# A planned two-layer encoder on one Trainium2 core: a later early group, its forms in the order of their use, a ScalarE copy and longer rests

## The chip, the cores and the metric

The kernel runs on one core of a Trainium2 chip. Its time is the device time of one execution in microseconds (us), and the figure to compare is the median of several runs. TensorE (PE) multiplies; VectorE (DVE), ScalarE (ACT) and GpSimd (POOL) do the rest; transfers are issued from the queue of SyncE (SP) and from that of POOL. The engines run asynchronously, each through its own queue in order, and wait for one another by semaphores.

## The reference

Two layers of a hybrid encoder for 256 tokens of width 2048. The part that matters here:

```python
h = rms_norm(x, norm_g)
u = h @ w_in                       # 4 branches' q, k, v, gates, an indexer, 4 x 2048 gate columns
y_a = sparse_index_attention(...)  # the indexer picks 64 keys a query
y_b = retention(...)
y_c = head_rms_norm(hgrn2(f, heads(c_i), heads(c_q)), hgrn_g)
y_m = memory_attention(...)
for n, (y, z) in enumerate(((y_a, a_z), (y_b, b_z), (y_c, c_z), (y_m, m_z))):
    branch = y.reshape(B, S, W).astype(dt) * jax.nn.silu(z)
    merged = merged + jax.nn.sigmoid(gate_all[:, :, n]) * (branch @ w_branch[n])
return x + merged @ w_out
```

All of it is float32, and weights dominate: each layer reads its own input projection (2048 x 15944), its branch projections and its output projection.

## The kernel before

**Arithmetic.** A float32 product is made of three passes in a reduced format: each operand is cut into a high part, which ScalarE rounds, and a low part, which VectorE subtracts, and TensorE adds high x high, high x low and low x high. Activations are the stationary operand, in 128 x 128 pieces; weights stream. The normalised input stands transposed in four blocks of four pieces, `x00`..`x03` in layer 0 and `x10`..`x13` in layer 1, each with an `h` and an `l` tile.

**Weights.** A slab is 512 rows x 512 columns (some 256 or 328 columns wide), loaded as `raw` by SP into one of four buffers. It is cut in two halves into `whi` and `wlo`, of which there are four each. `gemm_plan` fixes the order of all slabs in advance. `advance` follows each half that TensorE has been given: it pumps the stream and then cuts the half that comes four later. So the cast of that later half waits, on ScalarE's queue, for TensorE to have finished the half just issued.

**Tasks.** Everything beside the plain matmuls is a generator in `Stream.tasks`. `pump` counts a tick per half (half a tick for half a product, which is given twelve matmuls in two halves), sends up to five small transfers from `moves`, and lets tasks take up to two steps, in the order of their list, as long as `Account` (a ledger of estimated engine times) has VectorE and ScalarE no more than `LATE` = 2500 ns behind TensorE and the task's last step is over. `rest(n)` blocks a task for n ticks. `finish` is called where a result is needed: it runs the task to its end at once, whatever the ledger says, so its instructions stand in the queues ahead of the matmul that waits for them, and behind the cut of the last half.

**Folds.** `fold` transposes 32 x 32 blocks on VectorE (`xpi`, `cfi` and the like), then puts 16 transfers of 32 KB into `moves`, which go out alternately from POOL and SP, and rests five ticks. `turned` (L1416) does this for each quarter of the new residual between the layers with a rest of three ticks: when it resumes, `split_scaled` makes the block's high and low parts (four ScalarE and four VectorE instructions), and two squarings follow. The quarters 0 and 1 come out of the output projection together, 2 and 3 each four slabs later, and the next layer uses its blocks in the order 0, 1, 2, 0, 1, 2, 3, 3.

**Groups.** Some pairs of column chunks are computed as one seven-product group (a Winograd form of a 2 x 2 block product). The seven left operands (forms) are, in the order of use, r4, s3, a plain block, s1, s2 and two plain blocks: sums and differences of blocks of the scaled input, made by the task `forms` (L1212) in the order s1, s2, r4, s3 in one tile, each cut into an `h` and an `l` tile. The seven right operands are running sums of weight blocks (`sum`), four tiles a group: the first and the third stage are plain loads by SP, the others accumulating loads by POOL, issued as each stage has been cut. The sixth product (`i == RING`, the index from 0 being 5) takes plain slabs, and in the early group VectorE adds these to the chain. The early group gives the columns `ci` and `cz` of branch C. It is mingled with the slabs of the index and attention projections: `EARLY` = 4 slabs first, then products and slabs by `BETWEEN_PRODUCTS`. The loads of its first stage go out ten cuts ahead of its first. Groups for gate columns come later in both layers.

**Copies of the products.** All seven products go through the two halves of one PSUM tile (`px`): 0, 1, 0, 1, 1, 0, 1. `take` (L1299) issues a half product and, after the second, copies it out: by ScalarE, except the fifth (`i == 4`), which VectorE adds to `us` directly from PSUM. At the first product `take` calls `finish` on the whole of `forms`.

Of the kernel before, what the change touches and what calls it, by code (L numbers as in the profile page):

```python
# [153 lines left out]
GEN, HL, RAW = 23, 4, 4  # L154
DUO, AHEAD, FIRST, MERGED = (0, 3, 1), 10, 10, (0, 3, 2, 1)
STAGES = ((False, 1, 1), (True, 0, 1), (False, 0, 0), (True, 0, 1), (True, 1, 1))
LAST_SUM, RING, EARLY = (True, 1, 0), 5, 4
BETWEEN_PRODUCTS = (4, 3, 4, 4, 3, 2, 3)
MOVES, STEPS, BANKS, WARM = 5, 2, 2, 7
MARGIN, LATE = 500.0, 2500.0  # L160
# [2 lines left out]
class Stream:  # L163
# [51 lines left out]
            if t.done:  # L215
                self.tasks.remove(t)

    def finish(self, t):
        while not t.done:
            moved = t.step()  # L220
            if t.done:
                self.tasks.remove(t)
            elif not moved:
                ahead = self.tasks[:self.tasks.index(t)]
                if not any(u.step() for u in ahead):
                    self.tick()
                    self.idle += 1
                    assert self.idle < 1000
                self.tasks = [u for u in self.tasks if not u.done]
        return t.value  # L230
# [99 lines left out]
def wait_for(box, key):  # L330
    while key not in box:
        yield BLOCKED
    return box[key]
# [3 lines left out]
def trunk(ctx: ExitStack, tc: tile.TileContext, x, xt, memt, ng, qkg, hg, lbl, win, wmem, wbr, wout,  # L337
# [4 lines left out]
    ve, ac, po = (Counted(e, n, account) for e, n in ((nc.vector, "ve"), (nc.scalar, "ac"), (nc.gpsimd, "po")))  # L342
# [11 lines left out]
    def G(shape, name, dt=F32):  # L354
        return gen.tile(shape, dt, tag="g", name=name)
# [23 lines left out]
    stream, chains = Stream(account), {}  # L379
# [109 lines left out]
    def product(out, form, part, start, slabs):  # L489
        for h in (2 * part, 2 * part + 1):  # L490
            wh, wl = stream.parts.popleft()
            stream.used += slabs
            for k in range(2):
                fh, fl = form(2 * h + k)
                for i, (a, b) in enumerate(((fh, wh), (fh, wl), (fl, wh))):
                    te.matmul(out, a, b[:, k, :], start=start and h + k + i == 0, stop=h + k == 4 and i == 2,
                              skip_group_check=True)
            advance(0.5)
# [32 lines left out]
    def fold(cuts, nb, name, rest=5):  # L531
        inner = G([128, nb, 128], name + "i")
        at = 0
        for shape, src in cuts:
            n = int(np.prod(shape))
            part = inner[:, at:at + n, :]
            if len(shape) == 2:
                part = part.rearrange("p (a b) c -> p a b c", a=shape[0])
            ve.transpose(part, src)
            at += n  # L540
        yield
        whole = G([128, nb, 128], name)

        def move(q, a, b):
            q.dma_start(whole[b, :, a], inner[a, :, b])

        cut = [slice(32 * i, 32 * i + 32) for i in range(4)]
        left = [(a, b) for a in cut for b in cut]

        def moved(i):  # L550
            move((po, sy)[i % 2], *left.pop())

        stream.moves.extend([moved] * 16)
        while left:
            yield BLOCKED
        yield from stream.rest(rest)
        return whole

    def transposed(src, name, rest=5):
        u = yield from fold([((4, 2), src.rearrange("p t (h c) -> p h t c", h=4))], 8, name, rest)  # L560
        return u.rearrange("p (h t) c -> p h (t c)", h=4)
# [455 lines left out]
    hi = G([128, 4, 256], "memh", F32R)  # L1017
    lo = G([128, 4, 256], "meml", F32R)
# [147 lines left out]
    for l in range(L):  # L1166
# [45 lines left out]
        def forms(l=l):  # L1212
            rows = []
            for b in range(4):
                rows.append((yield from wait_for(rows_of, (l, b))))
            made = []

            def total(name, out, sign, first, second):
                for p in range(2):
                    at, a, b = (u[p] if isinstance(u, tuple) else u[:, 4 * p:4 * p + 4, :] for u in (out, first, second))  # L1220
                    yield
                    (ve.tensor_add if sign > 0 else ve.tensor_sub)(at, a, b)

            def parts(name, out):
                hi, lo = (spool.tile([128, 8, 128], F32R, tag="s", name=name + e) for e in "hl")
                yield
                ac.copy(hi, out)
                yield
                ve.tensor_sub(lo, out, hi.bitcast(F32))
                made.append((hi, lo))  # L1230

            a11, a12, a21, a22 = (tuple(rows[b + p][:, :, 128 * t:128 * t + 128] for p in range(2))
                                  for t in range(2) for b in (0, 2))
            one = G([128, 8, 128], "s1")
            yield from total("s1", one, -1, a21, a22)
            yield from parts("s1", one)
            yield from total("s2", one, -1, one, a11)
            yield from parts("s2", one)
            yield from total("r4", one, 1, one, a12)
            yield from parts("r4", one)  # L1240
            yield from total("s3", one, -1, a11, a21)
            yield from parts("s3", one)
            return made

        ready = [stream.add(forms())]
        early.append(rs)
        gemms(xh, [(win, l * DM * INW + CHUNK_AT[c]) for c in (O_CF, O_CQ)], 512, ["u", "u"], order=[(i, b, j) for i, b in PAIR_ORDER for j in range(2)],
              then=[scaled("uf"), scaled("uq")])
# [9 lines left out]
        def plain(b, t):  # L1258
            def form(k):
                return [u[:, k % 4, 128 * t:128 * t + 128] for u in xh[b + k // 4]]  # L1260
            return form

        def summed(i):
            def form(k):
                return [u[:, k, :] for u in ready[i]]
            return form

        groups, gates, open_gates = {}, {}, {}
# [1 line left out]
        def open_group():  # L1270
            stream.claim()
            return PB("px").rearrange("p (t n) -> p t n", t=2), {}, []

        def combined(parts, ended, first, second):
            qs, us = parts["qs"], parts["us"]
            ve.tensor_tensor(qs, qs, us[:, 0:1, :].to_broadcast([128, 2, 512]), op=OP.subtract)
            yield
            ve.tensor_tensor(us, qs, us[:, 1:2, :].to_broadcast([128, 2, 512]), op=OP.add)
            yield
            second = yield from second(us)  # L1280
            while not ended:
                yield BLOCKED
            one = parts["one"]
            ve.tensor_sub(one[:, 1, :], one[:, 1, :], qs[:, 1, :])
            yield
            first(one, 1, one[:, 1, :])
            return one, second
# [9 lines left out]
            return gate_path(us, rs, "cz")  # L1297

        def take(group, i, part):  # L1299
            if isinstance(ready[0], Task):  # L1300
                ready[:] = stream.finish(ready[0])
            if i == part == 0:
                groups[group] = open_group()
            ps, parts, ended = groups[group]
            first, second = (scale_rows, gated_path) if group == "c" else (sigmoid, both)
            to = ps[:, (0, 1, 0, 1, 1, 0, 1)[i], :]
            form = (summed(2), summed(3), plain(0, 0), summed(0), summed(1), plain(2, 0), plain(2, 1))[i]
            product(to, form, part, i != RING, i == RING)
            if not part:
                return  # L1310
            name = {0: "qs", 2: "us", RING: "one"}.get(i)
            if name:
                parts[name] = G([128, 2, 512], name)
            if i in (0, 2, 3, 6):
                name, t = {0: ("qs", 0), 2: ("us", 0), 3: ("us", 1), 6: ("one", 1)}[i]
                ac.copy(parts[name][:, t, :], to)
            elif i == 1:
                ac.activation(parts["qs"][:, 1, :], to, AF.Copy, scale=-1.0)
            elif i == RING:
                first(parts["one"], 0, to)  # L1320
            else:
                us = parts["us"]
                ve.tensor_add(us[:, 0, :], to, us[:, 0, :])
                task = stream.add(combined(parts, ended, first, second))
                gates[group, 2], gates[group, 3] = (task, 0), (task, 1)
            if i == 6:
                ended.append(True)
                del groups[group]
                stream.free()
# [84 lines left out]
                bridge(n, at[0], gates.pop((n, at[0])))  # L1414

        def turned(c, xc, nssq, l=l):  # L1416
            u = yield from transposed(xc, "xp", 3)
            r = split_scaled(u, ngs[:, l + 1, 4 * c:4 * c + 4], xtp, "xt", f"x1{c}")
            stream.add(scaling(u, l + 1, c))
            for t in range(2):  # L1420
                sq = G([128, 512], "xsq")
                ac.activation(sq, xc[:, t, :], AF.Square, accum_out=nssq[:, t * 4 + c:t * 4 + c + 1])
            return r
# [78 lines left out]
```

## Time and profile before

| what | value |
|---|---|
| median of three runs | 1845.88 us (1844.77 to 1848.36) |
| the profiled execution, its own time | 1853.45 us |
| its span, from the first to the last instruction | 1851.6 us |
| mean granted TensorE clock | 0.993 of full speed |
| DMA | 436.77 MB, mean 236 GB/s |
| accumulating loads on POOL (`sum`) | 120 of 512 KB, median 7.8 us from issue to landing |

A line of the timeline gives start, duration, engine, source line, operation, output<-inputs and shape; a bracket gives the idle time of the engine before it and what ended that. All matmuls share the line L145 and all compute of the other engines L127, because helper classes issue them, so instructions are told apart by their tiles. A matmul's duration is longer than the distance to the next, since matmuls overlap. A line of the windows gives busy time and number of instructions for PE, PEld (weight loads), DVE, ACT and POOL, then granted clock, DMA share and GB/s.

### The profile page before, as it was taken

What the parts mean: (1) busy time and instruction counts of PE and PEld (TensorE: products, weight loads), DVE (VectorE), ACT (ScalarE), POOL (GpSimd) and SP (SyncE); (2) the same over time, 40 slices, a digit from 0 to 9 for tenths busy, and PEclk for the clock granted to TensorE, in tenths of its full rate; (3) what the DMA queues carried; (4) which work ended last, traced back from release to release, by engine and by line L of the source; (5) the groups of instructions that cost most, each with busy time, mean ns of one, the idle gap of its engine ahead of it and who ended that gap; (6) DMA issues with size and microseconds to landing.
All of it is one profiled execution on the core that took longest, in us unless ns stands there. A gap on an engine that the chain in (4) does not pass through costs nothing. (4 is left out here: it accounts for less than half of the span.)

```text
span 1851.6 us, 24291 instructions
## 1 busy us (share of the span) xinstructions
PE 1824.5 (99%) x8884; PEld 1512.6 (82%) x8884; DVE 1314.5 (71%) x1422; ACT 1025.4 (55%) x1213; POOL 362.4 (20%) x525
## 2 busy tenths in 40 slices
PE   9999999999999999999999899999999999999999
PEld 7888878888888888888878787888888888888887
DVE  5666788886767667687655677888757666768764
ACT  5756555545555656555455555554555565655542
POOL 0021411151241011113121141113422101111310
PEclk9999999999999999999999899999999999999999
DMA  8779965787699899988797896566889989898774
GB/s 330 267 227 283 237 189 176 226 219 213 208 251 268 254 247 275 258 240 221 232 254 229 238 253 180 178 239 208 228 240 254 243 257 246 273 259 244 216 234 142
DMA packets 190600, 436.77 MB, mean 236 GB/s; under 512 B 114704, under 2 KB 115984, under 8 KB 156176
## 3 DMA queue, kind: packets, MB, share of 16 engines
q1 hardware_dynamic: 160624, 360.07, 59.4%
q0 software_dynamic: 29568, 74.87, 22.2%
q8 instruction: 70, 1.15, 0.3%
q14 instruction: 50, 0.41, 0.1%
q10 hardware_dynamic: 288, 0.26, 0.0%
HBM read 406.03 MB, written 5.24 MB: 222 GB/s over the span
## 5 line engine op out<-in xcount | busy, mean ns | idle before, releaser
L127 DVE TENSOR_TENSOR wlo<-raw,whi 128x1024 fp32r<-128x1024 f32 (+3 forms) x580 | 684.9, 1189 | 397.5 <-ACT whi L127 390.4
L127 ACT CAST whi<-raw 128x1024 fp32r<-128x1024 f32 (+3 forms) x580 | 594.2, 1028 | 628.1 <-PE u L145 402.7
L127 DVE TENSOR_TENSOR wlo<-sum,whi 128x1024 fp32r<-128x1024 f32 x192 | 231.5, 1223 | 79.7 <-ACT whi L127 71.0
L127 ACT CAST whi<-sum 128x1024 fp32r<-128x1024 f32 x192 | 201.2, 1055 | 111.2 <-PE u L145 55.2
L127 POOL DMA_DIRECT2D sum<-in_win x120 | 108.6, 905 | 609.3 <-DVE wlo L127 570.1
L145 PE MATMUL u<-wlo,x00h 128*128 128x512 f32 (+2 forms) x192 | 74.2, 387 | 0.4 <-DVE wlo L127 0.2
L145 PE MATMUL u<-whi,x00h 128*128 128x512 f32 (+2 forms) x192 | 74.2, 386 | 0.0
L145 PE MATMUL u<-whi,x11h 128*128 128x512 f32 (+2 forms) x192 | 74.0, 385 | 0.0
L145 PE MATMUL u<-whi,x02h 128*128 128x512 f32 (+2 forms) x192 | 73.9, 385 | 0.0
L145 PE MATMUL u<-wlo,x10h 128*128 128x512 f32 (+2 forms) x192 | 73.5, 383 | 0.4 <-DVE wlo L127 0.2
L145 PE MATMUL u<-whi,x00l 128*128 128x512 f32 (+2 forms) x192 | 73.8, 385 | 0.0
L145 PE MATMUL u<-whi,x01h 128*128 128x512 f32 (+2 forms) x192 | 73.8, 384 | 0.0
L145 PE MATMUL u<-whi,x03h 128*128 128x512 f32 (+2 forms) x192 | 73.7, 384 | 0.0
L145 PE MATMUL u<-whi,x12h 128*128 128x512 f32 (+2 forms) x192 | 73.6, 384 | 0.0
L145 PE MATMUL u<-wlo,x03h 128*128 128x512 f32 (+2 forms) x192 | 73.5, 383 | 0.0
L145 PE MATMUL u<-whi,x13h 128*128 128x512 f32 (+2 forms) x192 | 73.4, 382 | 0.0
L145 PE MATMUL u<-whi,x10h 128*128 128x512 f32 (+2 forms) x192 | 73.4, 382 | 0.0
L145 PE MATMUL u<-wlo,x01h 128*128 128x512 f32 (+2 forms) x192 | 73.3, 382 | 0.0
L145 PE MATMUL u<-wlo,x02h 128*128 128x512 f32 (+2 forms) x192 | 73.3, 382 | 0.0
L145 PE MATMUL u<-wlo,x11h 128*128 128x512 f32 (+2 forms) x192 | 73.3, 382 | 0.0
L145 PE MATMUL u<-wlo,x13h 128*128 128x512 f32 (+2 forms) x192 | 73.3, 382 | 0.0
L145 PE MATMUL u<-wlo,x12h 128*128 128x512 f32 (+2 forms) x192 | 73.3, 382 | 0.0
(490 smaller groups left out, 4399.9 us busy)
## 6 DMA issues: line engine op xcount, KB each, us to landing
raw<-in_win SPq DMA_DIRECT2D x192, 1024.0 KB, 5.9
sum<-in_win POOLq DMA_DIRECT2D x120, 512.0 KB, 7.8
sum<-in_win SPq DMA_DIRECT2D x64, 512.0 KB, 6.8
raw<-in_wbr SPq DMA_DIRECT2D x32, 1024.0 KB, 6.9
raw<-in_wout SPq DMA_DIRECT2D x32, 1024.0 KB, 5.9
raw<-in_wmem SPq DMA_DIRECT2D x12, 1024.0 KB, 4.9
raw<-in_win SPq DMA_DIRECT2D x8, 656.0 KB, 4.5
xc<-in_x SPq DMA_DIRECT2D x8, 512.0 KB, 6.9
```

Of the source, the lines that this page charges most:

```text
L127: return call(*args, **kw)
L145: return self.engine.matmul(out, w, x, **kw)
```

## The change

`EARLY` goes from 4 to 8, so that all eight slabs of the index projections come before the early group's first product; `gemm_plan`, which follows the same tokens, moves the group's loads with it. `forms` makes s1, s2 and r4 in three tiles, cuts r4 first, then makes s3 in r4's tile and cuts s3, s1 and s2; each finished form is entered in `made`. Its steps now yield behind the instruction instead of ahead of it. `take` waits for the one form that it needs, by `until`. The fifth product is copied by ScalarE into the free half of the tile `one`, which is now allocated here, and VectorE adds it to `us` from there; this holds for every group. `turned` rests five ticks for the quarters 0, 1 and 3, and three for quarter 2.

```diff
-LAST_SUM, RING, EARLY = (True, 1, 0), 5, 4
+LAST_SUM, RING, EARLY = (True, 1, 0), 5, 8
...
+    def until(self, t, enough):
+        self.finish(t, enough)
+
-    def finish(self, t):
-        while not t.done:
+    def finish(self, t, enough=None):
+        while not (enough() if enough else t.done):
...
-            def total(name, out, sign, first, second):
+            def total(out, sign, first, second):
                 for p in range(2):
                     at, a, b = (u[p] if isinstance(u, tuple) else u[:, 4 * p:4 * p + 4, :] for u in (out, first, second))
+                    (ve.tensor_add if sign > 0 else ve.tensor_sub)(at, a, b)
                     yield
-                    (ve.tensor_add if sign > 0 else ve.tensor_sub)(at, a, b)
...
-            one = G([128, 8, 128], "s1")
-            yield from total("s1", one, -1, a21, a22)
-            yield from parts("s1", one)
-            yield from total("s2", one, -1, one, a11)
-            yield from parts("s2", one)
-            yield from total("r4", one, 1, one, a12)
-            yield from parts("r4", one)
-            yield from total("s3", one, -1, a11, a21)
-            yield from parts("s3", one)
-            return made
+            s1, s2, r4 = (G([128, 8, 128], name) for name in ("s1", "s2", "r4"))
+            yield from total(s1, -1, a21, a22)
+            yield from total(s2, -1, s1, a11)
+            yield from total(r4, 1, s2, a12)
+            made["r4"] = yield from parts("r4", r4)
+            yield from total(r4, -1, a11, a21)
+            made["s3"] = yield from parts("s3", r4)
+            made["s1"] = yield from parts("s1", s1)
+            made["s2"] = yield from parts("s2", s2)
...
-            if isinstance(ready[0], Task):
-                ready[:] = stream.finish(ready[0])
+            name = ("r4", "s3", None, "s1", "s2", None, None)[i]
+            if name and name not in made:
+                stream.until(ready, lambda: name in made)
...
-            name = {0: "qs", 2: "us", RING: "one"}.get(i)
+            name = {0: "qs", 2: "us", 4: "one"}.get(i)
...
-                us = parts["us"]
-                ve.tensor_add(us[:, 0, :], to, us[:, 0, :])
+                us, spare = parts["us"][:, 0, :], parts["one"][:, 1, :]
+                ac.copy(spare, to)
+                ve.tensor_add(us, us, spare)
...
-            u = yield from transposed(xc, "xp", 3)
+            u = yield from transposed(xc, "xp", 3 if c == 2 else 5)
```

More of the change, by code (lines that the diff above doesn't have):

```diff
@@ L1215, in forms @@
                 rows.append((yield from wait_for(rows_of, (l, b))))
-            made = []
-            def total(name, out, sign, first, second):
+            def total(out, sign, first, second):
                 for p in range(2):
                     at, a, b = (u[p] if isinstance(u, tuple) else u[:, 4 * p:4 * p + 4, :] for u in (out, first, second))
+                    (ve.tensor_add if sign > 0 else ve.tensor_sub)(at, a, b)
                     yield
-                    (ve.tensor_add if sign > 0 else ve.tensor_sub)(at, a, b)
             def parts(name, out):
                 hi, lo = (spool.tile([128, 8, 128], F32R, tag="s", name=name + e) for e in "hl")
-                yield
                 ac.copy(hi, out)
@@ L1229, in parts @@
                 ve.tensor_sub(lo, out, hi.bitcast(F32))
-                made.append((hi, lo))
+                yield
+                return hi, lo
             a11, a12, a21, a22 = (tuple(rows[b + p][:, :, 128 * t:128 * t + 128] for p in range(2))
                                   for t in range(2) for b in (0, 2))
-            one = G([128, 8, 128], "s1")
-            yield from total("s1", one, -1, a21, a22)
-            yield from parts("s1", one)
-            yield from total("s2", one, -1, one, a11)
-            yield from parts("s2", one)
-            yield from total("r4", one, 1, one, a12)
-            yield from parts("r4", one)
-            yield from total("s3", one, -1, a11, a21)
-            yield from parts("s3", one)
-            return made
-        ready = [stream.add(forms())]
+            s1, s2, r4 = (G([128, 8, 128], name) for name in ("s1", "s2", "r4"))
[7 more added lines that the diff above has]
+            made["s2"] = yield from parts("s2", s2)
+        made = {}
+        ready = stream.add(forms())
         early.append(rs)
@@ L1264, in form @@
             def form(k):
-                return [u[:, k, :] for u in ready[i]]
+                return [u[:, k, :] for u in made[i]]
             return form
@@ L1306, in take @@
             to = ps[:, (0, 1, 0, 1, 1, 0, 1)[i], :]
-            form = (summed(2), summed(3), plain(0, 0), summed(0), summed(1), plain(2, 0), plain(2, 1))[i]
+            form = (summed("r4"), summed("s3"), plain(0, 0), summed("s1"), summed("s2"), plain(2, 0), plain(2, 1))[i]
             product(to, form, part, i != RING, i == RING)
```

## The prediction

> **What bounds the kernel now.** The page first.
>
> ```profile
> span 1851.6 us, 24291 instructions
> PE 1824.5 (99%) x8884; PEld 1512.6 (82%) x8884; DVE 1314.5 (71%) x1422; ACT 1025.4 (55%) x1213; POOL 362.4 (20%) x525
> PEclk9999999999999999999999899999999999999999
> ```
>
> TensorE is busy for 99% of the span, so nothing is won except where it stops: 1851.6 - 1824.5 = 27 us of idleness, and the slow matmuls behind it. One slice in 40 shows it in the granted clock. The waits of TensorE, longest first, begin with:
>
> ```profile
> PE px L145 <- ACT r4h L127: 8.6, 1, 8.6
> ```
>
> Now the timeline of TensorE around each stop. First the largest (**A**), where layer 1's early group begins:
>
> ```profile
> 1025.14 0.28 PE L145 MATMUL u<-whi,x13l 128*128 128x256 f32 x1
> 1033.99 0.80 PE L145 MATMUL px<-whi,r4h 128*128 128x512 f32 x1 [8.57 <-ACT r4h L127]
> ...
> 1038.59 0.39 PE L145 MATMUL px<-wlo,r4h 128*128 128x512 f32 x1
> 1038.82 0.39 PE L145 MATMUL px<-whi,r4l 128*128 128x512 f32 x1
> 1039.05 0.31 PE L145 MATMUL u<-whi,x10h 128*128 128x328 f32 x1
> ...
> 1042.65 0.39 PE L145 MATMUL px<-whi,r4h 128*128 128x512 f32 x1
> ```
>
> At full clock a 512-column matmul follows the last after 0.23 us, so half a product (12) takes 2.76. Here it takes 1039.05 - 1033.99 = 5.06: the stop also costs 2.30 of slow clock. With the start due at 1025.26, A is 8.73 + 2.30 = 11.0 us.
>
> **B**: the sixth product waits for VectorE to copy out the fifth product (`i == 4`; the change's "sixth form" is its `us` path), in both layers:
>
> ```profile
> 259.15 0.39 PE L145 MATMUL u<-whi,x02l 128*128 128x512 f32 x1
> 262.16 0.47 PE L145 MATMUL px<-whi,x02h 128*128 128x512 f32 x1 [2.61 <-DVE us L127]
> 266.30 0.63 PE L145 MATMUL u<-whi,x03h 128*128 128x512 f32 x1
> 272.07 0.39 PE L145 MATMUL px<-whi,x03h 128*128 128x512 f32 x1
> ...
> 1141.15 0.39 PE L145 MATMUL u<-whi,x12l 128*128 128x512 f32 x1
> 1143.88 0.58 PE L145 MATMUL px<-whi,x12h 128*128 128x512 f32 x1 [2.34 <-DVE us L127]
> 1148.30 0.39 PE L145 MATMUL u<-whi,x13h 128*128 128x512 f32 x1
> ```
>
> Layer 0: 2.78 stopped, 4.14 - 2.76 = 1.38 in the half product, 5.77 - 5.44 = 0.33 in the next slab (24 matmuls, 5.44 at full clock): 4.5. Layer 1: 2.50 + 4.42 - 2.76 = 4.2. B is 8.7.
>
> **C**, layer 0's second product, and **D**, the output projection of layer 0:
>
> ```profile
> 172.00 0.40 PE L145 MATMUL px<-whi,s3l 128*128 128x512 f32 x1
> 174.45 0.59 PE L145 MATMUL px<-whi,s3h 128*128 128x512 f32 x1 [2.05 <-ACT whi L127]
> ...
> 178.01 0.63 PE L145 MATMUL u<-whi,x00h 128*128 128x512 f32 x1
> ...
> 185.17 0.39 PE L145 MATMUL u<-whi,x01h 128*128 128x512 f32 x1
> ...
> 945.55 0.39 PE L145 MATMUL wo<-whi,mg0h 128*128 128x512 f32 x1
> ...
> 952.68 0.50 PE L145 MATMUL wo<-whi,mg3h 128*128 128x512 f32 x1 [1.53 <-ACT whi L127]
> 953.94 0.50 PE L145 MATMUL wo<-wlo,mg3h 128*128 128x512 f32 x1 [0.76 <-DVE wlo L127]
> ...
> 959.30 0.39 PE L145 MATMUL wo<-whi,mg2h 128*128 128x512 f32 x1
> ```
>
> C: 2.22 stopped, six matmuls in 3.56 for 1.38, a slab in 7.16 for 5.44: 6.1. D: 13.75 for two slabs of 5.44: 2.9. Together 28.7 us, and the profiled execution took 1853.45 (1851.6 and 1.85 around it), 7.6 above the median of 1845.88. I sum against the former and carry the difference over to the median. Of the four, C alone hangs on when a transfer lands, so it is the first candidate for those 7.6 us.
>
> **The change, part by part.**
>
> *Start four slabs later, forms in order of use (A).* Before, `take` calls `finish`, which issues all of s1, s2, r4, s3 at once while TensorE stands. After, r4 comes first, only r4 is waited for, and four 328-column slabs lie ahead.
>
> ```profile
> 1027.91 1.29 DVE L127 TENSOR_TENSOR s<-s,xp 128x512 f32<-128x512 f32 x2
> ...
> 1032.89 1.05 ACT L127 CAST r4h<-s 128x1024 fp32r<-128x1024 f32 x1 [2.62 <-DVE s L127]
> ```
>
> r4 needs three such pairs of sums (3.9) and a cast (1.05), with the low part behind it. A slab takes 1042.65 - 1039.05 = 3.60, so the cover grows by 14.4 us; a sum gets its turn about every second half slab, and eight steps want some 14 half slabs where 16 are there. A goes: **-11.0**. If the last two steps are still forced, some 2.5 us come back. The other forms (the same casts and subtractions) hide under later slabs: s3 has 16 us more. s1 and s2 keep two buffers longer: nothing visible, up to 1 us.
>
> *Copy by ScalarE (B).*
>
> ```profile
> 253.94 0.39 PE L145 MATMUL u<-whi,x02h 128*128 128x512 f32 x1
> ...
> 260.19 1.22 DVE L127 TENSOR_TENSOR sum<-sum,raw 128x1024 f32<-128x1024 f32 x1
> 261.33 0.68 DVE L127 TENSOR_TENSOR us<-px,us 128x512 f32<-128x512 f32 x1
> ...
> L127 ACT COPY us<-px 128x512 f32<-128x512 f32 x16 | 9.2, 575 | 0.0
> ```
>
> The product had ended when the slab of 253.94 began, but VectorE reached its sum at 261.33, behind low parts and chain sums. ScalarE's copy (0.58, eight in all, 4.6 us on an engine at 55%) stands behind one cast (1.06) and would end some 2 us after the product, with 5.4 us of slab as cover. The sum stays on VectorE, but frees no bank. So -8.7. What is late next: with 16 slabs to share instead of 20, no slab is left inside the sixth product (one was), and its four halves cost VectorE 4 x 2 x 1.22 = 9.8 us (a low part and a chain sum each) in a row with only 13.7 us of TensorE's work around them. With nothing else queued that just fits; a task's 1 to 3 us on top stops TensorE. Bounds 0 and the old 4.3 a layer; I take 1.5: **-8.7 + 3.0**.
>
> *The whole group moved (C).* Moved with it: the chains' first loads on SP (4 x 512 KB), the accumulating loads on POOL, the slabs' order. SP's loads now pass behind the first weights of the index projections; the folds' small transfers no longer start among the accumulations of the first product.
>
> ```profile
> 168.30 1.06 ACT L127 CAST whi<-sum 128x1024 fp32r<-128x1024 f32 x1 [2.87 <-DMA sum<-in_win]
> ...
> DMA to landing us min/median/max: 4.2/7.4/18.5
> ```
>
> The first product's sums landed late here. Its distance to the second product stays at 16.3 us (before two halves of 2.76 and three slabs of 3.60, after two halves and two of 5.44). Bounds -6.1 and +6.1 (it goes, or layer 1, without its 8.6 us of rest, gets one too). I take half the gain: **-3.0**.
>
> *Longer rest (D, and a new stop).* ScalarE was held 7.4 us by the split of x10, issued before its fold had landed:
>
> ```profile
> ACT x10h L127 <- DMA xp<-xpi: 7.4, 1, 7.4
> ...
> 975.82 1.06 ACT L127 CAST whi<-raw 128x1024 fp32r<-128x1024 f32 x1 [1.66 <-PE u L145]
> 977.83 1.72 ACT L127 ACTIVATE x12h<-xp,ngs 128x256 fp32r<-128x256 f32 x4 [0.96 <-DMA xp<-xpi]
> ...
> 981.06 0.39 PE L145 MATMUL u<-whi,x12h 128*128 128x512 f32 x1
> ```
>
> Two ticks (5.4 us) later, under 2 us of that hold are left, and weights are cut four halves ahead: D goes, -2.9. But x12 is ready only 2.6 us before its use. I carried the planner's ledger forward by hand: x10's split puts ScalarE over `LATE`, so no other step runs for a tick, and x12's fold begins one tick later, is held again by x11's split, and rests until two ticks later than before, one past its use. Then `finish` issues it behind a cast that waits for the half just used: 1.06 + 0.43 + latency, 1.8 us; then the low part behind VectorE's own cut, 0.8. I take **+2.9** (0 if a tick falls otherwise, 6 if its fold lands late as well). x13 comes out on the tick that it had.
>
> [...] After 2.34 us of idleness matmuls took 0.58 and 0.63 instead of 0.39, after 1.53 and 0.76 they didn't: these windows show it as granted clock.
>
> ```profile
> 950.00:960.00 10.00, 7.71 (x34) 5.80 (x33) 8.32 (x11) 8.66 (x16) 1.09 (x2) 1.00 0.75 215
> 1140.00:1150.00 10.00, 7.66 (x27) 5.84 (x26) 8.30 (x9) 3.15 (x3) 0.00 (x0) 0.83 0.76 293
> ```
>
> [...] The new stop of x12 lies between the two cases; taxed like B, it would be 1.7 more.
>
> **Sum**: -11.0 - 5.7 - 3.0 - 2.9 + 2.9 = -19.7 on 1853.45; carried to the median, 1845.9 - 19.7 = 1826.2. I add 0.8 for small waits (buffers): **1827.0**.
>
> **Rivals.**
> 1. *All four stops go, nothing new*: 1845.9 - 28.7 = 1817. For it: each cause is touched. Against it: x12's slack, and C may not exist in the timed runs. 0.10.
> 2. *VectorE becomes the group's bound.* The group's fourteen half products now share 16 slabs, not 20.
>
> ```profile
> 150.00:300.00 150.00, 144.66 (x836) 119.50 (x835) 114.17 (x143) 84.08 (x96) 39.41 (x56) 0.97 0.80 224
> ```
>
>    114 us of VectorE in 150; after, the group lasts 14.4 us less by its four slabs, and less again by its stops. If its tasks don't move out, B's stops return under another name (low parts instead of `us`) and C gives nothing: -11.0, 1835, to 1840 with x12 at its worst. Against it: tasks step only while it is under 2.5 us behind. 0.16.
> 3. *The wait only changes place*: r4 is still forced by late rows, or x13 too misses its tick, and B comes back: 1842 to 1849. Against it: 14.4 us of cover. 0.07.
> 4. *Slower: accumulating loads land late.* If landings pass the 16.3 us between a product and the next fed by it, which the slowest here (18.5) does, three products in each of two layers stop as C does: 6 x 6.1 = 36.6 against 22.6 won without C, 1860. It decides from about 5 such stops. For it: a DMA share near 1 around 150 to 175. Against it: the median landing, 7.4. 0.05.
>
> The forecast has 0.62 (1821 to 1833). Range: 1817 (rival 1) to 1841 (the far end of 2). A measurement of this kernel can tell about 0.2% (3.7 us) from no change: faster is forecast and rivals 1 and 2, 0.88; same 0.07; slower 0.05.
>
> **What would show it.** Right: no wait on r4h in layer 1; `px` no longer waits on DVE `us`; ScalarE without the 7.4 us hold before x10h; a stop of 2 to 3 us at the first matmul with x12h. Wrong: waits of `px` on DVE `wlo` in the sixth product (rival 2), casts of `sum` waiting for DMA while TensorE stands (rival 4), or the r4h wait back, smaller.

## The result, and the profile after

| | median | ratio to the kernel before, 95% interval |
|---|---|---|
| the changed kernel (6 runs) | 1834.03 us (1831.38 to 1836.02) | 0.9928 [0.9915, 0.994] |
| the kernel before beside it (6 runs) | 1847.12 us (1844.77 to 1848.89) | |

The change makes the kernel faster: 13.1 us between the medians, where 18.9 were forecast, and 1834.0 where 1827.0 was forecast. The profiled executions stand further apart: spans of 1851.6 and 1832.4, which is 19.2 us. The page after, and the first of its waits of TensorE:

```profile
span 1832.4 us, 24328 instructions
...
PE 1818.6 (99%) x8884; PEld 1509.4 (82%) x8884; DVE 1313.5 (72%) x1422; ACT 1025.5 (56%) x1221; POOL 359.7 (20%) x525
...
PEclk9999999999999999999999999999999999999999
```

```profile
PE u L145 <- DVE wlo L127: 2.8, 5, 1.3
PE u L145 <- ACT x12h L127: 1.5, 1, 1.5
...
PE ixrp L145 <- DVE cin L127: 1.1, 1, 1.1
...
PE u L145 <- DVE x12l L127: 0.5, 1, 0.5
```

A line of the waits names the waiting engine and tile, what it waited for, and us in total, times and the longest. The 8 in the row of the granted clock is gone, the wait of 8.6 us on r4h is gone, and no wait on `us` is left. TensorE's idleness is 1832.4 - 1818.6 = 13.8 us, before it was 27. The announced new stop at x12 is there.

To see where the 19.2 us come from, cut both traces at the same six pieces of work. First the kernel before, then the changed one, timeline of TensorE:

```profile
145.31 0.28 PE L145 MATMUL u<-whi,x03h 128*128 128x256 f32 x1
...
309.58 0.50 PE L145 MATMUL u<-whi,x01h 128*128 128x512 f32 x1
...
879.59 0.39 PE L145 MATMUL wo<-whi,mg0h 128*128 128x512 f32 x1
...
970.18 0.39 PE L145 MATMUL u<-whi,x10h 128*128 128x512 f32 x1
...
1002.82 0.39 PE L145 MATMUL u<-whi,x13h 128*128 128x512 f32 x1
...
1277.28 0.39 PE L145 MATMUL u<-whi,x13h 128*128 128x512 f32 x1
```

```profile
145.22 0.28 PE L145 MATMUL u<-whi,x03h 128*128 128x256 f32 x1
...
303.53 0.39 PE L145 MATMUL u<-whi,x01h 128*128 128x512 f32 x1
...
871.72 0.39 PE L145 MATMUL wo<-whi,mg0h 128*128 128x512 f32 x1
...
959.42 0.39 PE L145 MATMUL u<-whi,x10h 128*128 128x512 f32 x1
...
996.32 0.39 PE L145 MATMUL u<-whi,x13h 128*128 128x512 f32 x1
...
1256.85 0.48 PE L145 MATMUL u<-whi,x13h 128*128 128x512 f32 x1
```

The difference of two neighbours is the length of a stretch with the same matmuls in it, whatever their order:

| stretch | before | after | difference | forecast |
|---|---|---|---|---|
| layer 0's early group (from the last 256-column index slab to a slab of x01 behind the group) | 164.27 | 158.31 | -5.96 | B -4.5 + 1.5, C -3.0: -6.0 |
| the rest of layer 0, to the output projection | 570.01 | 568.19 | -1.82 | none |
| output projection (D) | 90.59 | 87.70 | -2.89 | -2.9 |
| six slabs on x10, x11, x12 | 32.64 | 36.90 | +4.26 | +2.9 |
| layer 1's early group, to a slab of x13 behind it | 274.46 | 260.53 | -13.93 | A -11.0, B -4.2 + 1.5: -13.7 |
| from there to the end of the span | 574.32 | 575.55 | +1.23 | +0.8 for small waits anywhere |

So on the execution that the sum was made for, the forecast of each stretch holds to within 2 us, and the whole to within 1. The new stop looks as it was drawn; ScalarE and TensorE after:

```profile
970.50 1.04 ACT L127 CAST whi<-raw 128x1024 fp32r<-128x1024 f32 x1 [1.66 <-PE u L145]
971.45 1.70 ACT L127 ACTIVATE x12h<-xp,ngs 128x256 fp32r<-128x256 f32 x4
```

```profile
964.86 0.39 PE L145 MATMUL u<-whi,x11h 128*128 128x512 f32 x1
...
972.01 0.50 PE L145 MATMUL u<-whi,x12h 128*128 128x512 f32 x1 [1.54 <-ACT x12h L127]
...
973.25 0.50 PE L145 MATMUL u<-whi,x12l 128*128 128x512 f32 x1 [0.51 <-DVE x12l L127]
...
980.00 0.39 PE L145 MATMUL u<-whi,x10h 128*128 128x512 f32 x1
```

The split of x12 stands behind the cast that waits for the half just used, its low part behind VectorE's own cut. Two slabs took 980.00 - 964.86 = 15.14 for 10.88: 4.26.

What stays open for the runs: which part of the change earns what; why the medians are nearer than the profiles; whether x12's stop can be had back.

### The profile page after: what moved, and what is told of

The parts are those of the page before. It is cut to its first block, busy times and chain, and to the rows that moved or that the text cites. A ratio compares the mean times of both kernels' runs of the same rounds, so it can differ in the third digit from the quotient of the medians.

```text
span 1832.4 us, 24328 instructions
## 1 busy us (share of the span) xinstructions
PE 1818.6 (99%) x8884; PEld 1509.4 (82%) x8884; DVE 1313.5 (72%) x1422; ACT 1025.5 (56%) x1221; POOL 359.7 (20%) x525
## 4 chain that ended last, share of the span: by engine, by line
PE 86%; DMA 5%; DVE 4%; issue 3%; ACT 1%; POOL 1%; SPq 0%; DVEq 0%; ACTq 0%; POOLq 0%
PE u L145 48%; PE px L145 12%; PE wo L145 9%; PE bw L145 9%; PE mv L145 2%; PE mk L145 2%; DVE wlo L127 2%; DMA sum<-in_win 2%; DMA cq<-cq0i 1%; ACT whi L127 1%; DMA aqpt<-aqpti 0%; DMA apT<-apT1i 0%; DVE sum L127 0%; PE ixrp L145 0%; DMA ixqt<-ixqti 0%
## 5 line engine op out<-in xcount | busy, mean ns | idle before, releaser
L145 PE MATMUL u<-whi,x12l 128*128 128x512 f32 (+2 forms) x192 | 73.8, 385 | 0.5 <-DVE x12l L127 0.5
L145 PE MATMUL u<-whi,x10l 128*128 128x512 f32 (+2 forms) x192 | 73.3, 382 | 0.0
```

Of the source, the lines that this page charges most:

```text
L145: return self.engine.matmul(out, w, x, **kw)
```

## The experiments

All stretches below are cut as in the table above (us of one profiled execution each). "Middle" is the rest of layer 0.

| kernel | group 0 | middle | out proj. | x10-x12 | group 1 | to the end |
|---|---|---|---|---|---|---|
| before | 164.27 | 570.01 | 90.59 | 32.64 | 274.46 | 574.32 |
| before, again | 161.28 | 573.79 | 88.83 | 32.65 | 274.40 | 574.25 |
| rests alone | 159.77 | 571.98 | 87.71 | 35.31 | 274.73 | 574.29 |
| copy alone | 156.09 | 570.92 | 89.57 | 32.64 | 271.80 | 574.26 |
| start alone | 158.15 | 568.19 | 89.31 | 32.64 | 268.38 | 583.99 |
| start and order | 157.57 | 568.20 | 89.10 | 32.64 | 258.28 | 584.29 |
| changed | 158.31 | 568.19 | 87.70 | 36.90 | 260.53 | 575.55 |
| changed, again | 157.72 | 568.20 | 87.70 | 36.10 | 259.79 | 575.28 |
| changed, third | 158.01 | 568.19 | 87.71 | 36.87 | 259.08 | 579.41 |
| changed, rests of 3 | 157.49 | 568.20 | 89.23 | 32.64 | 259.00 | 585.07 |
| changed, VectorE copies | 157.86 | 568.19 | 87.70 | 35.31 | 259.13 | 576.63 |
| changed, start as before | 154.78 | 569.88 | 87.70 | 35.28 | 266.85 | 575.25 |
| changed, rest of 2 for x12 | 157.77 | 568.21 | 87.70 | 34.88 | 261.62 | 577.94 |
| rests 5, 5, 2, 2, recall 6 | 157.99 | 570.96 | 87.70 | 34.51 | 259.28 | 575.52 |

### One part of the change alone

The kernel before, with the ScalarE copy:

```diff
-            name = {0: "qs", 2: "us", RING: "one"}.get(i)
+            name = {0: "qs", 2: "us", 4: "one"}.get(i)
...
-                us = parts["us"]
-                ve.tensor_add(us[:, 0, :], to, us[:, 0, :])
+                us, spare = parts["us"][:, 0, :], parts["one"][:, 1, :]
+                ac.copy(spare, to)
+                ve.tensor_add(us, us, spare)
```

> The kernel before with the copy of the fifth product by ScalarE alone. Theory 1 (the stops are separate and each is worth in timed runs what the trace of before shows): the two waits of px on DVE us go, 4.5 + 4.2 = 8.7 us, less at most 1 us of waits for low parts: 7.7 to 8.7 us faster, ratio 0.9953 to 0.9958. Theory 2 (the 6 us that are missing between the spans, 19.2 us shorter, and the medians, 13.1 us lower, were lost here, VectorE's queue holding TensorE up under another name): 2 to 4 us faster, with new waits of px or u on DVE wlo around the sixth product.

Measured: 1841.80 us, ratio 0.9954 [0.9939, 0.9968]. That is theory 1's ratio, but in part by luck. Layer 1's group wins 2.7 us (274.5 to 271.8): 4.0 around the sixth product, less 0.6 for a wait on `wlo` behind it and 0.6 by which the stop on r4h was dearer in this execution. Layer 0's group wins 5.7 against a mean of 161.8, and in this execution C happened to be cheap (1.5 us). The kernel before, with the longer rests:

```diff
-            u = yield from transposed(xc, "xp", 3)
+            u = yield from transposed(xc, "xp", 3 if c == 2 else 5)
```

> The kernel before with the longer rests alone. Theory 1: the stop in the output projection goes (-2.9) and the new stop before x12 comes (+4.3, as in the trace after: 980.00 - 964.86 less two slabs of 5.44): 1.4 us slower, ratio 1.0008, and ScalarE's 7.4 us before x10h is gone. Rival: the stop before x12 belongs to the moved group and not to the rests: 2.9 us faster, ratio 0.9984, without a wait on x12h.

Measured: 1851.04 us, ratio 0.9998 [0.9989, 1.0008]. The wait on x12h is there, so it belongs to the rests and the rival falls; theory 1's ratio is at the end of the interval. The changed kernel with copy and rests put back, which leaves the later start and the order of the forms:

> The kernel after with the copy and the rests put back: only the later start, the new order of the forms and the wait for one form. Theory 1: the wait on r4h goes, 11.0 us, and the 6.1 us of layer 0's second product are not in the timed runs of before, so 8 to 11 us faster, ratio 0.994 to 0.9957. Theory 2 (that stop is in all runs of before and goes too): 14 to 17 us faster, ratio 0.991 to 0.9925.

Measured: 1835.43 us, ratio 0.9918 [0.9904, 0.9932]. That is theory 2's range, but not its sum, which had no B in it: against the second profile of before, layer 1's group alone wins 274.40 - 258.28 = 16.1 us (A and B together), and the last stretch loses 10.0. And the kernel before, profiled once more on the same chip:

> The kernel before, unchanged, profiled once more. Theory 1: the stop of px at 172 us (waits on whi and wlo, 6.1 us with its slow clock) is small or absent and the execution takes 1845 to 1849 us; the stops on r4h and on us are there with 8 to 9 and 2 to 3 us. Theory 2: the stop at 172 us is there again and the execution takes some 1853 us, so that profiling itself adds the 6 us.

Measured: 1851.51 us for that execution. Neither theory holds as it stands: the second product of layer 0 stands again (1.95 + 0.77 us), but 1851.51 is close to 1851.07, the median of the kernel before beside it, so profiling adds nothing that shows. C is no accident of one execution; only its price varies, as the last section shows.

The ratios add up to -0.46 - 0.02 - 0.82 = -1.30%, more than the change has. So the parts overlap, and the waits of TensorE say where. Copy alone, rests alone, and start and order alone, the first waits of each:

```profile
PE px L145 <- ACT r4h L127: 8.6, 1, 8.6
PE u L145 <- DVE wlo L127: 1.5, 4, 0.7
```

```profile
PE px L145 <- ACT r4h L127: 8.6, 1, 8.6
PE px L145 <- DVE us L127: 4.9, 2, 2.6
PE u L145 <- ACT x12h L127: 1.5, 1, 1.5
```

```profile
PE mov L145 <- DVE mpl L127: 3.9, 1, 3.9
PE alg L145 <- DVE ay L127: 1.7, 1, 1.7
```

Of the four stops, the copy removes the wait on `us` (B) alone; waits of 0.7 us and less on `wlo` stand in its place. The rests win 1.1 us in the output projection against the second profile of before and 2.9 against the first (88.83 and 90.59 to 87.71), and lose 2.67 at x12 (35.31 - 32.64), about a draw. Start and order remove the wait on r4h, and also the wait on `us`, though VectorE still copies the fifth product out there: it now gets to it in time. They have a cost of their own: a wait of `mov` on `mpl`, of which more below.

### One part taken out of the change

The changed kernel again, on the chip of the next three runs:

> The changed kernel itself, so that it stands beside the group's move alone (1835.43 us) and its own parts on one chip. Theory 1 (the parts overlap: the move of the group alone frees both B and the r4h stop, the copy then has nothing left to win, the longer rests give back with x12 what D wins): a ratio to the kernel before of 0.990 to 0.993, within 3 us of the group's move alone. Theory 2 (the parts add, and the first comparison was disturbed): 0.987, as copy 0.9954 times rests 0.9998 times group 0.9918.

Measured: 1832.14 us, ratio 0.9909 [0.9892, 0.9925]. Theory 1 holds: the whole is no better than its largest part by more than a few us.

VectorE copies the fifth product again:

```diff
-            name = {0: "qs", 2: "us", 4: "one"}.get(i)
+            name = {0: "qs", 2: "us", RING: "one"}.get(i)
...
-                us, spare = parts["us"][:, 0, :], parts["one"][:, 1, :]
-                ac.copy(spare, to)
-                ve.tensor_add(us, us, spare)
+                us = parts["us"]
+                ve.tensor_add(us[:, 0, :], to, us[:, 0, :])
```

> The changed kernel with VectorE copying the fifth product out again. Theory 1 (VectorE is early enough once the group's start is moved): no wait of px on DVE us above 0.5 us, time within 2 us of the changed kernel. Theory 2 (the copy is what removes B): waits on us of 2.3 to 2.6 a layer are back, 5 to 9 us slower than the changed kernel.

Measured: 1832.72 us, ratio 0.991 [0.9891, 0.993], with no wait on `us` among TensorE's. Theory 1: behind the later start the copy by ScalarE is worth nothing that can be measured.

Rests of 3 for all four quarters again:

```diff
-            u = yield from transposed(xc, "xp", 3 if c == 2 else 5)
+            u = yield from transposed(xc, "xp", 3)
```

> The changed kernel with the rest of every x1 row block at 3 again. Theory 1: the x12 stop (4.3 us in the changed kernel's trace: 980.00 - 964.86 - 2 x 5.44) is gone, the output projection loses some 1 us (0.8 in the group's move alone), so 2 to 4 us faster than the changed kernel. Theory 2 (the rests win D and cost nothing net): the same or up to 3 us slower, with ScalarE's hold before x10h back at 6 to 7 us in both cases.

Measured: 1836.46 us, ratio 0.9933 [0.9915, 0.9951]: 4.3 us slower than the changed kernel between the medians, where theory 1 said 2 to 4 faster and theory 2 at most 3 slower. The first half of theory 1 came true: the stretch x10-x12 is back at 32.64, 3.5 shorter than beside it, and the output projection 1.5 longer. But the last stretch is 585.07 instead of 575.28, +9.8. `alg` waits 1.7 us there for `ay` (0.2 in the changed kernel), and the larger stop is this one; timeline of TensorE, then a wait of VectorE:

```profile
1415.29 0.58 PE L145 MATMUL mov<-mpl,mvhi 128*128 128x256 f32 x1 [4.24 <-DVE mpl L127]
```

```profile
DVE mpl L127 <- DMA apT<-apT1i: 5.6, 1, 5.6
```

From the end of the stop on, matmuls of 512 columns follow one another after 0.43 us instead of 0.23 and those of 256 after 0.21 instead of 0.12: twenty take 6.28 us (1415.29 to 1421.57) where 11 x 0.12 + 9 x 0.23 = 3.39 would do, 2.9 more; with 1.5 more at `alg` and 4.2 at `mov` that is 8.6 of the 9.8. This is layer 1's memory branch, 440 us behind x12. Its low part `mpl` stands on VectorE's queue until the fold of another branch (`apT`) has landed. With the longer rests the tasks get their turns in another order: the transfers of `apT` leave SP from 1371.3 on and those of `mpT` from 1394.5, with rests of 3 `mpT` goes first, from 1373.4, and `apT` from 1389.9, and only there is the stop. The same stretch is as long in both other kernels with the later start and rests of 3 (584.29 and 583.99). So the rests pay, but not by D, for which they were costed: they pay by a stop 440 us later. Why `mpl` waits for a fold that doesn't feed it wasn't tried; both take their tiles from one ring of 23 buffers (`GEN`), so a shared buffer would do it, but no run shows that.

### The stop at x12

A rest of 2 for x12 alone:

```diff
-            u = yield from transposed(xc, "xp", 3 if c == 2 else 5)
+            u = yield from transposed(xc, "xp", 2 if c == 2 else 5)
```

> The changed kernel with a rest of 2 instead of 3 for x12 alone, so that its split is issued one tick (2.7 us) earlier, ahead of the cast that it stood behind. Theory 1 (x12's stop is the one tick of lateness): the wait of u on x12h falls from 1.5 us to under 0.5, the stop from 4.3 us to at most 1.5, and the time is 2 to 4 us under the changed kernel. Theory 2 (the fold itself lands late, so the tick doesn't matter): ScalarE waits for the DMA of xp in place of the cast, the stop stays at 3 to 5 us and the time is the same.

Measured: 1838.20 us, ratio 0.9941 [0.9921, 0.9962], 6.1 us slower than the changed kernel. The split of x12 came a tick earlier as meant, and x13 was caught in its place; TensorE:

```profile
970.36 0.50 PE L145 MATMUL u<-whi,x12h 128*128 128x512 f32 x1 [0.15 <-ACT x12h L127]
...
994.04 0.50 PE L145 MATMUL u<-whi,x13h 128*128 128x512 f32 x1 [1.54 <-ACT x13h L127]
...
995.29 0.50 PE L145 MATMUL u<-whi,x13l 128*128 128x512 f32 x1 [0.51 <-DVE x13l L127]
```

Neither theory said so: x12's own wait is gone, as theory 1 had it, but the stop comes again four slabs later. In the table, the first of the two waits at x13 falls into the stretch x10-x12 and the second into group 1. Its profile took only 3.7 us longer than the one beside it, so the rest of the 6.1 isn't explained here.

Rests chosen so that no split is overtaken by its use, and a later start of recall, so that the two folds of layer 1 end in the order of the changed kernel:

```diff
-        yield from stream.rest(2)
+        yield from stream.rest(6)
...
-            u = yield from transposed(xc, "xp", 3 if c == 2 else 5)
+            u = yield from transposed(xc, "xp", (5,5,2,2)[c])
```

> The changed kernel with rests of 5, 5, 2, 2 for the row blocks 0 to 3 and with a first rest of 6 instead of 2 in recall, so that in layer 1 the fold of the last scores of attend ends ahead of that of recall, the other way round than where mov stopped. Theory 1 (x12's stop and the mov stop are two separate costs, each of a fold that is forced or late): neither stop is there, x12h waits under 0.3 us and mov on mpl under 0.5, and the time is 3 to 5 us under the changed kernel. Theory 2 (a wait only changes its place whenever the order moves): one of at least 3 us is there under another name, and the time is within 2 us of the changed kernel or above it.

Measured: 1832.87 us, ratio 0.9914 [0.99, 0.9928], beside the changed kernel's 1832.38. This is nearer to theory 2: the stop of `mov` is not there, but x12h waits as before, and the time is the same. ScalarE there, then with rests of 3 for all:

```profile
972.86 1.71 ACT L127 ACTIVATE x12h<-xp,ngs 128x256 fp32r<-128x256 f32 x4 [2.56 <-DMA xp<-xpi]
```

```profile
968.35 1.71 ACT L127 ACTIVATE x12h<-xp,ngs 128x256 fp32r<-128x256 f32 x4 [0.86 <-DMA xp<-xpi]
```

No cast is ahead of the split now; x12's fold itself lands late. Behind rests of 5 for x10 and x11 the last of its transfers leave SP by 968.3, behind rests of 3 by 963.5. The kernel with a rest of 2 for x12 alone has the same rests ahead of x12. There the split also waited for the fold (1.22 us), but began 10.63 us behind the first matmul with x10h (969.79 - 959.16), and here 11.97 (972.86 - 960.89). So behind the forced split stands the fold, which lands just when x12 is used: 0.15 us late in the one, 1.49 in the other. A new wait in layer 0 (`alg` on `ay`, 2.5 us) took what was left. Neither attempt beat the changed kernel.

### Start and order of the group

The kernel before, with `EARLY` at 8 alone:

```diff
-LAST_SUM, RING, EARLY = (True, 1, 0), 5, 4
+LAST_SUM, RING, EARLY = (True, 1, 0), 5, 8
```

> The kernel before with EARLY at 8 alone: the early group starts four slabs later, its forms still in the order s1, s2, r4, s3, and VectorE still copies the fifth product out. In layer 1 the r4 sums now have slabs to hide behind, but r4's cast, its low part and the whole of s3 are still issued at the first product (7 steps, where before it were 14). Theory 1 (the four slabs take most of A, the order takes the rest): an r4h wait of 2 to 5 us is left of 8.6, and no wait on us above 0.7, since the group's start alone frees the sixth product; a ratio of 0.992 to 0.996. Theory 2 (the order of the forms is what removes A): r4h waits 6 us or more, ratio 0.995 to 1.0.

Measured: 1844.96 us, ratio 0.9971 [0.9961, 0.9981]. The changed kernel with `EARLY` at 4 again:

> The changed kernel with EARLY at 4 again: order of the forms, copy by ScalarE and rests stay, the group starts where it did. By r4's three last steps (half a sum 0.65, cast 1.05, low part 1.23, and a first half of s3 that doesn't feed r4) TensorE should stop 3 to 5 us at r4h instead of 8.6. Theory 1 (order and start each take a part of A): r4h wait 3 to 5 us, 4 to 8 us slower than the changed kernel. Theory 2 (the start alone decides): 7 us or more, 9 to 12 us slower. Either way C may show at the second product of layer 0 again, with up to 6 us; if it doesn't, the start of the group isn't what removes it.

Measured: 1838.35 us, ratio 0.994 [0.9927, 0.9954]. And the changed kernel a third time beside them:

> The changed kernel once more, as the measure for the three runs beside it: 1830 to 1835 us, ratio 0.990 to 0.993, with x12h as its longest wait, 1.5 to 3.1 us.

Measured: 1832.38 us, ratio 0.9904 [0.9889, 0.9919]. Its longest wait is not x12h, as was expected, but one of 2.7 us on `qs`, a copy of a product (see the rivals below). The waits on r4h with the start alone, then with the order alone:

```profile
PE px L145 <- ACT r4h L127: 5.8, 1, 5.8
```

```profile
PE px L145 <- ACT r4h L127: 4.0, 1, 4.0
```

With the order alone it is theory 1 (4.0 us of wait, 6.0 slower). The start alone lies between the theories: 5.8 is above the 2 to 5 of theory 1 and just under the 6 of theory 2, and 0.9971 is in theory 2's range, though 9.7 us of its time are the last stretch with the stop of `mov`. Of A, four slabs alone take about a third of the wait and the order half of it; only together does r4 fit in ahead of its product. The order alone costs 6.0 us against the changed kernel's median, and its profile shows 266.85 - 259.08 = 7.8 in layer 1's group.

Layer 0's group goes the other way: 154.78 with the old start, 157.5 to 158.3 in all eight with `EARLY` at 8 and the new order. With the old start C didn't come back either, so the start can't be all that removes C; in one profile, and with a cost that varies as much as C's, no more follows.

## Why the prediction was right, and where it was not

**A, -11.0: right in mechanism and size.** The wait on r4h is gone, and the first r4 product starts on time:

```profile
1032.97 0.31 PE L145 MATMUL u<-whi,x13l 128*128 128x328 f32 x1
1033.12 0.40 PE L145 MATMUL px<-whi,r4h 128*128 128x512 f32 x1
```

Layer 1's group gave 13.93 where A and B together were forecast at 13.7. The cover of 14.4 us alone would not have done it, as the start alone showed: the order was the other half.

**B, -8.7: right in size, the cause only half.** The copy removes the stop when it is made alone, though a wait on `wlo` takes some of the gain back; behind the later start there is nothing left for it (with the start alone, a wait of 0.4 us on `us` is all there is). The prediction costed the copy in the old place and the move without it, and so never saw that one gain had two owners. For the whole that makes no difference, for the parts it makes all.

**New waits around the sixth product, +1.5 a layer: mis-sized in both.** In layer 1 they are two, 0.85 us together (0.34 and none in the other two profiles of the changed kernel):

```profile
1132.65 0.50 PE L145 MATMUL px<-wlo,x13h 128*128 128x512 f32 x1 [0.24 <-DVE wlo L127]
...
1134.92 0.50 PE L145 MATMUL u<-wlo,x10h 128*128 128x512 f32 x1 [0.61 <-DVE wlo L127]
```

In layer 0 they are not in the sixth product but elsewhere in the group:

```profile
159.74 0.42 PE L145 MATMUL u<-wlo,x03h 128*128 128x328 f32 x1 [0.46 <-DVE wlo L127]
...
208.68 0.50 PE L145 MATMUL u<-wlo,x01h 128*128 128x512 f32 x1 [1.33 <-DVE wlo L127]
...
273.11 1.91 PE L145 MATMUL ixrp<-ixkt,ixqt 64*32 64x128 f32 x64 [1.12 <-DVE cin L127]
```

The middle one has VectorE held by a fold (`cq` waits 2.55 us for its transfers, the cut of the next low part stands behind it). These three are 2.9 us together, and layer 0's group is 158.31 - 154.78 = 3.5 us above the run with the old start. The term was 1.5, and 0.8 for small waits.

**C, -3.0: right for the median, wrong for the profile that it was summed on.** The profiled execution had all of C, and all of it went. But in four profiles of kernels that are alike up to that point, C cost 6.1, 3.3, 1.7 and 1.5 us (stop and slow matmuls from the second half product to the end of the next slab, as the prediction counts them), a mean of 3.1. Half is what an ordinary run holds, but it was taken as the half of a gain that was either there or not, so its fit is luck. In the table, group 0 falls by 5.96 against the first profile, by 2.97 against the second (161.28 - 158.31) and by 1.46 against the third. That the whole stretch met its forecast of -6.0 is two errors that cancel: twice the gain from C, and some 2 to 3 us more of new waits.

**D, -2.9: right on that execution, large for an ordinary one.** ScalarE's hold of 7.4 us before x10h is gone:

```profile
ACT x11h L127 <- DMA xp<-xpi: 1.7, 1, 1.7
...
ACT x10h L127 <- DMA xp<-xpi: 0.3, 1, 0.3
```

The stretch is 87.70, and where the rests are 3 it is 88.83 to 90.59 in six profiles: 1.1 to 2.9.

**x12, +2.9: right in mechanism, mis-sized.** The stops themselves were 1.54 + 0.51 = 2.05 us where 2.6 were forecast; with the slow matmuls that follow in some executions, the price was 4.26, 3.46 and 4.23 in the three profiles of the changed kernel (in the second it is one stop of 3.11) and 2.67 where VectorE copies. The 1.7 that the prediction put beside it as the tax would have made it 4.6.

**The carry to the median: the step that failed.** 7.6 us of the profiled execution lay above the median of the runs shown, and the sum, made against the former, was taken whole off the latter. The prediction looked for them in C first, as the one stop that hangs on a landing; but D hangs on one as well, that of x10's fold. The kernel before varies in just the stretches that the change clears: group 0 (159.8 to 164.3), the output projection, and the middle, 570.0 to 573.8 in four profiles, where `mov` waits for `mpl` (0.28 us in the first profile, 1.96 in the second), `alg` for `ay` (0.56) and in two of them a half product for `qs` (1.35 and 1.26). In eight of the nine with the new start none of these waits is there and it is 568.2; the ninth has `alg` again, with 2.46. That last gain is in no term of the forecast. The means of the stretches, before (of those profiles in the table in which the part at stake is still as before) against the three of the changed kernel: group 0 161.8 to 158.0, middle 571.7 to 568.2, output projection 89.4 to 87.7, x10-x12 32.6 to 36.6, group 1 274.5 to 259.8, the end 574.3 to 576.8. That is -3.8 - 3.5 - 1.7 + 4.0 - 14.7 + 2.5 = -17.2 where the forecast has -18.9, and two of the three comparisons measured 17.1 (1849.2 to 1832.1, 1849.5 to 1832.4). In the first it was 13.1 (1847.1 to 1834.0). So the mechanisms carry the gain, some 2 us too much of it; the rest of the 7 us by which 1827.0 is too low is the base: the three runs shown have a median of 1845.88, and 1847.1, 1851.1, 1849.2 and 1849.5 were the medians of the kernel before in the four comparisons. Why it was lowest in the first wasn't settled.

**The rivals.** VectorE didn't become the bound (0.85 us of waits around layer 1's sixth product, 2.9 in layer 0's group), and the forms are not late. The slowest sum lands sooner (14.6 us, before 18.5; median 8.0, before 7.4), so rival 4 didn't come; but ScalarE's casts of `sum` waited 22.6 us in all for landings, 10.8 before. In the third profile of the changed kernel such a wait reached TensorE, in a later group of layer 1:

```profile
1397.81 1.04 ACT L127 CAST whi<-sum 128x1024 fp32r<-128x1024 f32 x1 [3.95 <-DMA sum<-in_win]
1398.76 0.59 ACT L127 ACTIVATE qs<-px 128x512 f32<-128x512 f32 x1
...
1399.40 0.50 PE L145 MATMUL px<-whi,x10h 128*128 128x512 f32 x1 [2.65 <-ACT qs L127]
```

The copy `qs` stands behind the late cast, and TensorE waits for the copy. Behind it eight matmuls follow one another after 0.43 us instead of 0.23 (3.41 us from 1400.69 to 1404.10 where 8 x 0.23 = 1.84 would do), 1.6 more; with the 2.65 that is about the 4.1 us by which the last stretch is longer there than in the second profile. All four stops did go, and something new came, as forecast.

**The rests** were costed as a draw, and alone they are one (0.9998). Inside the change they are worth 4.3 us, by the stop of `mov` in layer 1 that the later start brings and the rests take away. Nothing in the profile of before shows that stop.

## What to carry to other kernels

Sum a forecast by stretches between fixed pieces of work, and carry to the median only what the median holds: profile the kernel before more than once, and where a stretch differs between executions, take its mean length. When two edits can remove the same wait, cost each alone and both together, or the parts add up to more than the whole. In a kernel whose tasks take turns by a ledger, a rest changes the order of everything behind it; look for its price hundreds of us later too, and don't expect a stop that is pushed away by a tick to be gone.

A kernel with `EARLY` at 4 in layer 0 and 8 in layer 1 suggests itself (154.78 against 158.3 in the one, 266.85 against 259.1 in the other); it wasn't tried.

## What the runs showed of the hardware

The same stop doesn't cost the same. The windows of 16 us around the second product of layer 0, in the kernel before and in its second profile; PEclk is third from the right:

```profile
170.00:186.00 16.00, 13.28 (x47) 10.21 (x46) 10.79 (x14) 9.99 (x13) 0.64 (x1) 0.79 0.83 315
```

```profile
170.00:186.00 16.00, 13.29 (x58) 10.41 (x57) 12.25 (x16) 10.43 (x13) 2.56 (x4) 1.00 0.84 307
```

TensorE stood 2.05 + 0.67 us in the first and 1.95 + 0.77 in the second. The granted clock fell to 0.79 in the one, and C cost 6.1; it stayed at 1.00 in the other, and C cost 3.3. At x12 the stops of 1.54 + 0.51 us came with 0.89 in the changed kernel and with 1.00 in the one where VectorE copies:

```profile
968.00:984.00 16.00, 13.94 (x53) 10.69 (x52) 6.49 (x8) 9.49 (x17) 3.16 (x6) 0.89 0.74 178
```

```profile
968.00:984.00 16.00, 13.94 (x61) 10.87 (x60) 7.55 (x9) 9.71 (x17) 3.65 (x7) 1.00 0.72 202
```

The price was 4.26 and 2.67. In the second profile of the changed kernel one stop of 3.11 us at x12h left the clock at 1.00.

Narrower windows show what these means are made of. In the changed kernel:

```profile
974.00:978.50 4.50, 4.50 (x14) 3.50 (x14) 0.77 (x2) 1.84 (x5) 0.00 (x0) 0.62 0.95 257
```

Windows of 0.4 us read 1.00 up to 974.0, 0.90 in the first, 0.50 in each of the eight from 974.4 to 977.6, 0.84 in the next and 1.00 from 978.0 on, so the clock stood at 0.50 for some 4.5 x 0.38 / 0.5 = 3.4 us. In it eight matmuls follow one another after 0.43 us instead of 0.23, 3.37 us from 974.28 to 977.65 where 8 x 0.23 = 1.84 would do: 1.5 more, and 4.26 - 2.67 is 1.6. Around C, the clock from 174 to 183 is 0.62 in the mean and 0.50 in each 0.4 us from 174.8 to 181.2, by the same sum 9 x 0.38 / 0.5 = 6.8 us, twice as long, and 6.1 - 3.3 is 2.8. The prediction's row behind B (0.83 over 10 us) gives 3.4 once more. In these executions a stop cost its length and 0.35 to 0.6 us more (3.46 for 3.11, 2.67 for 2.05), and in some of them slow matmuls beside that: 1.6 us where the clock stood at 0.50 for 3.4 us, 2.8 where it did for 6.8.

So the prediction read too much into single rows when it took 2.34 us as taxed and 1.53 + 0.76 as free: here the length of a stop alone doesn't decide it. The clock fell behind 1.54 + 0.51 us of idleness with 0.73 us of work between them in the changed kernel, and stayed at 1.00 behind the same where VectorE copies, and behind 3.11 in one piece. What does decide it, no run shows.
